# An encoder layer with two kinds of attention: projections as one stream through all head pairs, a shared bank for short score stretches, and a fixed order on three engines

## The chip, the cores and the metric

The kernel runs on one core of a Trainium2 chip. The metric is the device time of one execution in microseconds (us), the median of several. One execution was also profiled, and the trace below is of that one. The engines are PE (TensorE: matrix products and transposes), DVE (VectorE), ACT (ScalarE), POOL (GpSimd) and SP (SyncE, which issues transfers). Each runs its own instructions in the order of its own list, and stands still when the next one's data or room is not there.

## The reference

One encoder layer on two streams of tokens, `x_prompt` (1024 tokens, called R here) and `x_sample` (512 tokens, S), with shared weights. Eight heads of width 64 do neighbourhood attention on a grid (group a), eight do dilated window attention (group b).

```python
hn = rms_norm(x, g_attn)
proj = hn @ w_in
qa, ka, va, qd, kd, vd = jnp.split(proj, 6, axis=-1)
oa = neighbourhood_attention(heads(qa), heads(ka), heads(va), rpb)
od = dilated_attention(heads(qd), heads(kd), heads(vd), slopes)
mix = jnp.concatenate([rms_norm(oa, g_na), rms_norm(od, g_dil)], axis=-1)
x = x + mix @ w_out
hn = rms_norm(x, g_ffn)
return x + (jax.nn.silu(hn @ w_gate) * (hn @ w_up)) @ w_down
```

Inside each attention, a block of 128 queries meets its window of keys: scores, plus a table of biases and masks, softmax over the window, times the values.

## The kernel before

**Pairs and blocks.** Attention goes through 16 pairs: two heads of one group and one stream. Pairs 0 to 7 are those of R (b, a, b, a, ...), pairs 8 to 15 those of S in the same order. A pair of R has 16 blocks, eight of its first head and then eight of its second; a pair of S has four and four. `blocks_of(pi)` lists them, and `k.j` is the number of a block within its head.

**One block.** Scores are two sorts of product into a bank of PSUM, L698 with the high part of the keys and L699 with the low part (`sc`; in a b block of R a long stretch of 512 keys and a short one of 256, of which the short one had the name `sc2`; 384 keys in an a block of R; 512 and 256 in the b and a blocks of S). DVE adds the table and takes the minimum of the negated scores (L739, with the reading of its accumulator). ACT takes the exponential (L746). PE transposes the result (L756, bank `tp`), ACT copies it as 16-bit numbers (L760, the high part of `pT`), DVE computes what the copy lost (L761, the low part). PE multiplies with the values (L776), two blocks at a time, DVE adds up their pieces (L785), and after four blocks it takes the reciprocal and POOL scales and stores.

**Projections.** The queries, keys and values of the next pair are computed while a pair's blocks are (`qkv(pi)`, a generator; order v, q, k). Each product of an fp32 activation and an fp32 weight is three products of rounded halves (`mm3`, L155); the generator yields after every six, which is called a step here. A pair of R costs 24 steps, 144 matmuls of 512 columns; one of S 12 steps, 72 matmuls. Behind the matmuls come works of DVE, ACT and POOL: the sums `am` (L426) and low parts of v (L473), q (L539) and k (L508), ACT's high parts and copies, and, for b, copies at the borders (L411, L412).

**What sets the order.** `interleave()` writes one pair's blocks and the next pair's projections alternately: scores one block ahead, `dense.upto((j + DF) / n)` in the middle of block j and `dense.upto((j + 1) / n)` at its end, with `j` counted over all `n` blocks of the pair. That is only the order in which the program is written: the scheduler of the language then sets each engine's order, by data and by priorities, so that an engine's list can hold a later block's work ahead of an earlier one's. Only the opening (first loads and projections) is written in a fixed order. `bank()` hands out PSUM banks by name: 2 for projections (`mm`), 3 for scores (`sc`), 1 for values, 2 for transposes.

**Tables.** The bias tables of group a are built from `bias_e` tiles that `bias_load` loads and `bias_rows` (L332 to L339) shifts and writes back; they take their room in turn from the tag `p16`, which also serves the 16-bit values. Attention lies between some 67 and 795 us of the trace; after it follow the output projection's rest and the feed-forward part, which the change does not touch.

## Time and profile before

| what | value |
|---|---|
| median of 3 runs | 1977.09 us (1970.92 to 1977.22) |
| profiled execution | 1966.33 us, span of the trace 1964.3 us |
| PE busy over the span | 1842.0 us (94%) |
| DVE, ACT, POOL busy | 1321.1, 916.4, 844.1 us (67%, 47%, 43%) |
| PE's share of the chain that ended last | 74% |
| DVE's, DMA's share of it | 9%, 7% |

The span is the time from the first instruction of the trace to the last; the execution's own time is a little more. The busy shares are means over stages with different limits. The chain that ended last is followed back from the last instruction: at each step to what released it, or to the instruction before it on its engine. The granted clock in the rows below (PEclk) is TensorE's: 1.00 stands for its upper level of 2.4 GHz, 0.50 for its lower of 1.2 GHz.

### The profile page before, as it was taken

Reading aid. Unit: us, or ns where it says so; the run is one execution under the profiler, and the core shown is the slowest. Engines: PE = TensorE matmul, PEld = TensorE weight load, DVE = VectorE, ACT = ScalarE, POOL = GpSimd, SP = SyncE. Lnnn points to the kernel's source line nnn. Section 1 sums busy time; section 2 is a strip of 40 time slices with the busy share of each in tenths; the row PEclk is TensorE's granted clock in tenths of the full one; section 3 lists DMA queues with packets and bytes.
Section 4 is the critical chain, followed back from the end, with each engine's and each line's share of the span. In section 5 each row is a group of like instructions: output and inputs, shape, how many; then the busy total and the mean of one; then the engine's idle time right before and its main releaser. Section 6 shows DMA issues by size and latency. Waiting matters only on the chain.

```text
span 1964.3 us, 28970 instructions
## 1 busy us (share of the span) xinstructions
PE 1842.0 (94%) x10450; PEld 1609.9 (82%) x10450; DVE 1321.1 (67%) x2626; ACT 916.4 (47%) x1731; POOL 844.1 (43%) x690
## 2 busy tenths in 40 slices
PE   6889999898999998999899999879999997999998
PEld 4777777677777776788899999879999995877886
DVE  7566656656656567566976777877767665757765
ACT  5455557555566667443433333433333332324431
POOL 4323324232355551100666666656666543642110
PEclk9999999999899998999999999989999998999999
DMA  7623323232344455353354343334343448866642
GB/s 263 142 66 99 88 82 104 58 88 69 97 108 119 117 164 143 136 161 118 107 150 130 108 131 101 113 109 122 105 131 104 132 127 314 272 217 234 226 166 94
DMA packets 218943, 265.97 MB, mean 135 GB/s; under 512 B 59584, under 2 KB 163152, under 8 KB 218800
## 3 DMA queue, kind: packets, MB, share of 16 engines
q1 hardware_dynamic: 196176, 179.57, 30.4%
q0 software_dynamic: 22624, 84.56, 14.5%
q8 instruction: 82, 1.34, 0.3%
q14 instruction: 61, 0.50, 0.1%
HBM read 202.71 MB, written 51.41 MB: 129 GB/s over the span
## 4 chain that ended last, share of the span: by engine, by line
PE 74%; DVE 9%; DMA 7%; issue 4%; ACT 3%; POOL 2%; SPq 0%; DVEq 0%; POOLq 0%; ACTq 0%
PE acc L155 37%; PE yacc L155 11%; PE zacc L155 7%; PE mmacc L155 7%; PE pt L756 4%; PE pv L776 3%; PE sc L698 2%; DVE flo L1080 2%; PE sc L699 2%; DMA left<-hid_d 1%; DMA fraw<-in_w_up_dram 1%; POOL fs L1084 1%; DVE t L739 1%; PE pt L210 1%; DMA wq<-in_w_down_dram 1%
## 5 line engine op out<-in xcount | busy, mean ns | idle before, releaser
L155 PE MATMUL acc<-dhi,left 128*128 128x512 f32 x924 | 289.8, 394 | 16.6 <-ACT left L1254 14.0
L155 PE MATMUL acc<-hth,whi 128*128 128x512 f32 x576 | 233.5, 405 | 7.1 <-DVE kl L508 5.4
L155 PE MATMUL acc<-htl,whi 128*128 128x512 f32 x576 | 231.3, 401 | 1.0 <-POOL htl L294 0.5
L1080 DVE TENSOR_TENSOR flo<-fs,fhi 128x512 fp32r<-128x512 f32 x176 | 173.8, 991 | 86.2 <-ACT fhi L1079 85.1
L155 PE MATMUL acc<-hth,wlo 128*128 128x512 f32 x576 | 230.5, 400 | 0.1
L155 PEld LDWEIGHTS acc<-dhi,left 128*128 128x128 f32 x924 | 174.1, 189 | 57.8 <-ACT left L1254 15.3
L1079 ACT ACTIVATE fhi<-fs 128x512 fp32r<-128x512 f32 x176 | 109.5, 629 | 188.3 <-POOL fs L1084 81.4
L125 POOL TENSOR_TENSOR wlo<-wraw,whi 128x1024 fp32r<-128x1024 f32 x48 | 115.7, 2411 | 165.9 <-ACT whi L124 154.8
L155 PE MATMUL acc<-dlo,left 128*128 128x512 f32 x462 | 181.5, 393 | 0.0
L746 ACT ACTIVATE t<-t,mt 128x768 f32<-128x768 f32 (+3 forms) x192 | 138.1, 720 | 68.5 <-DVE mt L739 64.4
L760 ACT ACTIVATE pT<-pt 128x512 f16<-128x512 f32 (+2 forms) x256 | 118.8, 485 | 108.3 <-PE pt L756 107.1
L1084 POOL TENSOR_TENSOR fs<-fraw 128x512 f32<-128x512 f32 x88 | 131.6, 1510 | 83.6 <-DMA fraw<-in_w_up_dram 76.6
L1080 DVE TENSOR_TENSOR flo<-fraw,fhi 128x512 fp32r<-128x512 f32 x132 | 160.4, 1216 | 0.3 <-ACT fhi L1079 0.2
L1238 POOL TENSOR_TENSOR wq<-wq 128x512 f32<-128x512 f32 x55 | 92.3, 1689 | 156.7 <-DMA wq<-in_w_down_dram 124.5
L761 DVE SCALAR_TENSOR_TENSOR pT<-pt,pT 128x512 f16<-128x512 f32 (+2 forms) x256 | 136.8, 550 | 14.0 <-ACT pT L760 13.0
L1079 ACT ACTIVATE fhi<-fraw 128x512 fp32r<-128x512 f32 x132 | 82.9, 629 | 115.0 <-PE yacc L155 92.4
L155 PEld LDWEIGHTS acc<-hth,whi 128*128 128x128 f32 x576 | 109.9, 191 | 31.2 <-DVE kl L508 6.9
L756 PE MATMUL pt<-ident,t 128*128 128x128 f32 x768 | 125.6, 283 | 6.2 <-DVE pT L761 5.0
L1255 DVE TENSOR_TENSOR left<-left,left 128x1408 fp32r<-128x1408 f32 x42 | 74.4, 1773 | 83.8 <-ACT left L1254 83.8
L155 PEld LDWEIGHTS acc<-htl,whi 128*128 128x128 f32 x576 | 110.1, 191 | 24.9 <-DVE htl L294 2.1
L791 POOL TENSOR_TENSOR ob<-ob,den 128x256 f32<-128x256 f32 x48 | 29.6, 617 | 234.1 <-DVE ob L785 99.5
L1198 POOL TENSOR_TENSOR as<-a,as 128x384 f32<-128x384 f32 x66 | 89.0, 1348 | 91.9 <-DVE a L1187 72.5
(219 smaller groups left out, 4980.7 us busy)
## 6 DMA issues: line engine op xcount, KB each, us to landing
wq<-in_w_down_dram SPq DMA_DIRECT2D x132, 256.0 KB
hid_d<-as POOLq DMA_DIRECT2D x22, 1344.0 KB, 8.0
left<-hid_d SPq DMA_DIRECT2D x42, 704.0 KB
wraw<-in_w_in_dram POOLq DMA_DIRECT2D x46, 512.0 KB, 5.0
fraw<-in_w_gate_dram SPq DMA_DIRECT2D x45, 512.0 KB
fraw<-in_w_up_dram SPq DMA_DIRECT2D x45, 512.0 KB
tabb<-in_tabb_dram POOLq DMA_DIRECT2D x8, 800.0 KB, 4.9
xh<-x_d SPq DMA_DIRECT2D x12, 512.0 KB
```

Source lines behind the costliest of these rows:

```text
L125: eng.tensor_tensor(out=lo, in0=src, in1=hi.bitcast(F32), op=ALU.subtract))
L155: latest[0] = nc.tensor.matmul(out=out, lhsT=a, rhs=b, start=first and i == 0, stop=i == last, skip_group_check=not first)
L746: nc.scalar.activation(t, t, AF.Exp, bias=mt, scale=-1.0, accum_out=k.den)
L756: nc.tensor.transpose(out=pt[:, c * P:(c + 1) * P], in_=k.t[:, (c0 + c) * P:(c0 + c + 1) * P], identity=ident)
L760: nc.scalar.activation(hi, pt, AF.Copy, scale=16384.0)
L761: nc.vector.scalar_tensor_tensor(out=lo, in0=pt, scalar=16384.0, in1=hi, op0=ALU.mult, op1=ALU.subtract)
L1079: nc.scalar.activation(hi, src, AF.Copy)
L1080: nc.vector.tensor_tensor(out=lo, in0=src, in1=hi.bitcast(F32), op=ALU.subtract)
L1084: nc.gpsimd.tensor_tensor(out=o, in0=a, in1=b, op=op)
L1198: nc.gpsimd.tensor_tensor(out=part[n], in0=p, in1=q, op=op)
L1238: nc.gpsimd.tensor_tensor(out=src, in0=src, in1=other, op=q[1])
L1255: nc.vector.tensor_tensor(out=lo, in0=raw_lo, in1=hi.bitcast(F32), op=ALU.subtract)
```

## The change

`interleave()` and its class `Dense` go. In their place all blocks of all pairs stand in one list `todo`, and all projections in one generator `stream()`. `step(g)` writes block g: its softmax, the transposes, copies and low parts of the block before (`turn(pipe[-1])`), the sums and values of earlier ones, the scores of block g+1, and then as many steps of projections as `target(k.pi, k.j)` asks for, meant to run `LEAD` = 2 blocks ahead. Ahead of a new pair's first scores the stream is drained until that pair's projections are "whole". Where the pair whose projections stream (`at[0]`) is none of 4, 7, 15 and 16, the three engines PE, ACT and DVE keep the order in which the program is written (`manual_schedule`); that is while the blocks of pairs 0, 1, 2, 4, 5, 7 and 8 to 13 run. Pairs 3, 6, 14 and 15 are left to the scheduler.

Besides: the short stretch of a b block of R takes half of one bank of its own (`s2`), the halves in turn, and `sc` has two banks instead of three; the second head's low keys have two tiles in turn (`klow`), so that `held`, which delayed them, goes; the low parts of both heads are issued together (`lows`); the high part of v's second half comes three steps later; the `bias_e` tiles take the room of the tag `pT`; values are taken at odd `j`.

```diff
-TB, P16, PTB, OB = 3, 3, 3, 2
-BANKS = dict(mm=("mm", 2), sc=("sc", 3), pv=("pv", 1), tp=("tp", 2))
+TB, P16, PTB, OB = 3, 2, 3, 2
+BANKS = dict(mm=("mm", 2), sc=("sc", 2), s2=("s2", 1), pv=("pv", 1), tp=("tp", 2))
...
-            f = rb.tile([P, NA + 1, 32], F32, tag="p16", name="bias_e", bufs=P16)
+            f = rb.tile([P, NA + 1, 32], F32, tag="pT", name="bias_e", bufs=PTB)
...
-                    v_high_a(1)
+                    after(3, lambda: v_high_a(1))
...
-                res["kl"] = [z[:, :nx] for z in klow]
+                res["kl"] = [klow[i][:, :nx] for i in (0, 1 + pi % 2)]
...
-                sc = bank("sc", "sc2")
+                if "s2" not in heads:
+                    heads["s2"] = bank("s2", "s2")
+                sc = heads["s2"][:, k.j % 2 * 256:k.j % 2 * 256 + 256]
...
+    totals = [12 * st.nch for st, _, _ in pairs] + [11 + 8 * NO]
+    counts = [2 * st.nq for st, _, _ in pairs]
...
+    def target(pi, j):
+
+        base, j = sum(totals[1:pi + 1]), j + 1 + LEAD
+        if pi == len(pairs) - 1:
+            return base + totals[pi + 1] * j / (counts[pi] + LEAD)
+        if j <= counts[pi]:
+            return base + totals[pi + 1] * j / counts[pi]
+        n = counts[min(pi + 1, len(pairs) - 1)] + (LEAD if pi + 2 == len(pairs) else 0)
+        return base + totals[pi + 1] + totals[pi + 2] * (j - counts[pi]) / n
...
+    def step(g):
+        k = todo[g]
+        softmax(k)
+        if pipe:
+            turn(pipe[-1])
+        pipe.append(k)
+        while owed:
+            head_out(owed.pop())
+        if k.j % 2 and len(pipe) > LAG:
+            values(pipe[:2])
+            owed.append(pipe[1])
+            del pipe[:2]
+        if g + 1 < len(todo):
+            nxt = todo[g + 1].pi
+            while not done.get(nxt, {}).get("whole"):
+                advance()
+            scores(todo[g + 1])
+        if g + TL < len(todo):
+            tables(todo[g + TL])
+        while spent[0] < target(k.pi, k.j):
+            was = spent[0]
+            advance()
+            if spent[0] == was:
+                break
...
+    loose = (SQ, len(order) - 1, len(pairs) - 1, len(pairs))
+    g = 0
+    while g < len(todo):
+        with ExitStack() as fixed:
+            if at[0] not in loose:
+                fixed.enter_context(tc.manual_schedule(engines=core))
+            now = at[0] in loose
+            while g < len(todo) and (at[0] in loose) == now:
+                step(g)
+                g += 1
```

In the rows of order below, a name's number tells one use of a buffer from another, and `ISA` is the score operation that adds the table. DVE in the second head of pair 0, before (score operations are L739, low parts L761):

```order
L739 ISA t_1050,mt_1051<-sc_994,tabb_799 128x512
L739 ISA mt_1051 128x1
L739 ISA t_1050,mt_1053<-sc2_997,tabb_799,mt_1051 128x256
L739 ISA mt_1053 128x1
L761 SCALAR_TENSOR_TENSOR pT_981<-pt_982,pT_981 128x512
L761 SCALAR_TENSOR_TENSOR pT_981<-pt_989,pT_981 128x256
L739 ISA t_1105,mt_1106<-sc_1027,tabb_799 128x512
L739 ISA mt_1106 128x1
L761 SCALAR_TENSOR_TENSOR pT_1014<-pt_1015,pT_1014 128x512
L785 TENSOR_REDUCE ob_1012<-pv_718 128x128
L761 SCALAR_TENSOR_TENSOR pT_1014<-pt_1022,pT_1014 128x256
L739 ISA t_1105,mt_1108<-sc2_1030,tabb_799,mt_1106 128x256
```

And after (score operations L741, low parts L763):

```order
L741 ISA t_1037,mt_1038<-sc_1032,tabb_838 128x512
L741 ISA mt_1038 128x1
L741 ISA t_1037,mt_1040<-s2_557,tabb_838,mt_1038 128x256
L741 ISA mt_1040 128x1
L763 SCALAR_TENSOR_TENSOR pT_1043<-pt_1044,pT_1043 128x512
L763 SCALAR_TENSOR_TENSOR pT_1043<-pt_1051,pT_1043 128x256
L787 TENSOR_REDUCE ob_982<-pv_700 128x128
L790 RECIPROCAL den_751<-den_751 128x4
L741 ISA t_1066,mt_1067<-sc_1061,tabb_838 128x512
L741 ISA mt_1067 128x1
L741 ISA t_1066,mt_1069<-s2_557,tabb_838,mt_1067 128x256
L741 ISA mt_1069 128x1
```

Before, the scores of the blocks `t_1006`, `t_1050` and `t_1105` stand together, and the low parts `pT_981` and `pT_1014` belong to blocks three back. After, between the scores of two blocks stand always the two low parts of the block before the first of them.

ACT at the same place, before (exponentials are L746, copies L760):

```order
L746 ACTIVATE t_1050,den_955<-t_1050,mt_1053 128x768
L760 ACTIVATE pT_1014<-pt_1015 128x512
L760 ACTIVATE pT_1014<-pt_1022 128x256
L760 ACTIVATE pT_1080<-pt_1081 128x512
L746 ACTIVATE t_1105,den_955<-t_1105,mt_1108 128x768
L760 ACTIVATE pT_1080<-pt_1088 128x256
L746 ACTIVATE t_1153,den_1158<-t_1153,mt_1156 128x768
L760 ACTIVATE pT_1116<-pt_1117 128x512
L760 ACTIVATE pT_1116<-pt_1124 128x256
L760 ACTIVATE pT_1184<-pt_1185 128x512
L746 ACTIVATE t_1211,den_1158<-t_1211,mt_1214 128x768
```

And after (L748 and L762):

```order
L762 ACTIVATE pT_995<-pt_1003 128x256
L748 ACTIVATE t_1037,den_967<-t_1037,mt_1040 128x768
L762 ACTIVATE pT_1043<-pt_1044 128x512
L762 ACTIVATE pT_1043<-pt_1051 128x256
L748 ACTIVATE t_1066,den_967<-t_1066,mt_1069 128x768
L762 ACTIVATE pT_1072<-pt_1073 128x512
L762 ACTIVATE pT_1072<-pt_1080 128x256
L748 ACTIVATE t_1114,den_1119<-t_1114,mt_1117 128x768
L762 ACTIVATE pT_1121<-pt_1122 128x512
L762 ACTIVATE pT_1121<-pt_1129 128x256
L748 ACTIVATE t_1141,den_1119<-t_1141,mt_1144 128x768
```

Before, one to three pairs of copies stand between exponentials, and a pair of copies is also split by one. After, it is one exponential and the copies of one block in strict turn, and the block whose copies follow an exponential is the one before it.

PE at the end of pair 0, before; `acc` are projections, `sc` scores of pair 1, `pt` transposes of pair 0's last blocks:

```order
L155 MATMUL acc_1347<-hth_100,wlo_1246 128x512
L155 MATMUL acc_1347<-hth_100,whi_1245 128x512
L698 MATMUL sc_1341<-ka0_1147,qa0_879 128x384
L699 MATMUL sc_1341<-kl0_92,qa0_879 128x384
L155 MATMUL acc_1347<-htl_101,whi_1245 128x512
L155 MATMUL acc_1347<-hth_100,wlo_1246 128x512
L756 MATMUL pt_1227<-ident_69,t_1153 128x128 x2
L776 LDWEIGHTS pT_1184
L776 MATMUL pv_718<-vnb_463,pT_1184 128x64
L776 LDWEIGHTS pT_1184
```

And after; the rows left out are 56 further projection matmuls and one small product:

```order
L778 MATMUL pv_700<-vnb_465,pT_1200 128x64
L778 LDWEIGHTS pT_1200
L778 MATMUL pv_700<-vnb_465,pT_1200 128x128
L155 MATMUL acc_883<-hth_104,whi_638 128x512
L155 MATMUL acc_883<-htl_105,whi_638 128x512
L155 MATMUL acc_883<-hth_104,wlo_639 128x512
...
L155 MATMUL acc_1352<-htl_103,whi_1330 128x512
L155 MATMUL acc_1352<-hth_102,wlo_1331 128x512
L698 MATMUL sc_1361<-ka0_1309,qa0_846 128x384
L699 MATMUL sc_1361<-kl0_92,qa0_846 128x384
L758 MATMUL pt_1375<-ident_69,t_1223 128x128 x4
L758 MATMUL pt_1382<-ident_69,t_1223 128x128 x2
```

Before, the first scores of pair 1 stand amid the projections, and transposes and values of pair 0 behind them. After, 60 projection matmuls stand in one piece between the last values that pair 0's loop takes and the first scores of pair 1; in the eight blocks of the second head ahead of them PE's list has no projection matmul at all.

## Rows read from the trace of the kernel before

The windows of rows 1 run from the first score operation of a pair to that of another: pair 0, pair 2, pair 7, and pairs 8 to 13.

**Rows 1.** Windows: us; busy PE, PEld, DVE, ACT, POOL; PEclk; DMA share; GB/s.
```profile
67.00:148.00 81.00, 69.39 (x448) 55.47 (x447) 44.54 (x119) 42.39 (x83) 22.05 (x25) 0.96 0.52 117
202.10:278.70 76.60, 72.84 (x507) 59.03 (x507) 50.55 (x127) 44.71 (x91) 23.22 (x27) 0.96 0.27 71
534.10:588.40 54.30, 53.17 (x345) 42.67 (x345) 28.47 (x81) 34.47 (x77) 29.69 (x24) 1.00 0.42 107
588.40:742.20 153.80, 147.78 (x955) 118.80 (x953) 97.39 (x259) 102.79 (x229) 78.91 (x77) 0.99 0.50 136
```

**Rows 2.** Waits of TensorE for a bank: us in total, times, longest.
```profile
PE sc L698 <- DVE mt L739: 19.5, 23, 5.6
```

**Rows 3.** Timeline of VectorE, two score operations: start, us.
```profile
375.45 0.69 DVE L739 CUSTOM_DVE_ANT_0 t<-sc,tabb 128x512 f32<-128x512 f32 x1 [0.76 <-PE pt L756]
...
378.66 0.69 DVE L739 CUSTOM_DVE_ANT_0 t<-sc,tabb 128x512 f32<-128x512 f32 x1 [1.04 <-PE pt L756]
```

**Rows 4.** Groups by shape, 48 to 800 us: busy, mean ns; idle, releasers.
```profile
L761 DVE SCALAR_TENSOR_TENSOR pT<-pt,pT 128x512 f16<-128x512 f32 x96 | 65.2, 686 | 6.1 <-ACT pT L760 5.8
L739 DVE CUSTOM_DVE_ANT_0 t<-sc,tabb 128x512 f32<-128x512 f32 x96 | 65.1, 687 | 47.4 <-PE pt L756 46.7
L746 ACT ACTIVATE t<-t,mt 128x768 f32<-128x768 f32 x64 | 59.8, 934 | 51.7 <-DVE mt L739 50.0 <-DVE den L788 1.1
L760 ACT ACTIVATE pT<-pt 128x512 f16<-128x512 f32 x96 | 56.3, 594 | 37.3 <-PE pt L756 36.8
...
L785 DVE TENSOR_REDUCE ob<-pv 128x128 f32<-128x256 f32 x94 | 39.5, 420 | 26.8 <-PE pv L776 17.6 <-issue 8.5
L761 DVE SCALAR_TENSOR_TENSOR pT<-pt,pT 128x256 f16<-128x256 f32 x95 | 39.3, 416 | 4.1 <-ACT pT L760 3.9
L746 ACT ACTIVATE t<-t,mt 128x384 f32<-128x384 f32 x64 | 39.3, 614 | 7.2 <-DVE mt L739 5.7 <-DVE den L788 0.3
...
L760 ACT ACTIVATE pT<-pt 128x256 f16<-128x256 f32 x95 | 35.6, 377 | 38.5 <-PE pt L756 38.3
...
L739 DVE CUSTOM_DVE_ANT_0 t<-sc,taba 128x384 f32<-128x384 f32 x64 | 35.0, 553 | 49.1 <-PE pt L756 48.1 <-PE sc L699 0.5
L761 DVE SCALAR_TENSOR_TENSOR pT<-pt,pT 128x384 f16<-128x384 f32 x64 | 34.7, 548 | 3.7 <-ACT pT L760 3.4
...
L539 DVE SCALAR_TENSOR_TENSOR qa<-acc,qa 64x512 fp32r<-64x512 f32 x46 | 31.7, 688 | 22.7 <-ACT qa L535 21.9
...
L760 ACT ACTIVATE pT<-pt 128x384 f16<-128x384 f32 x64 | 30.2, 484 | 32.4 <-PE pt L756 32.0
...
L739 DVE CUSTOM_DVE_ANT_1 t<-sc,tabb,mt 128x256 f32<-128x256 f32 x48 | 22.9, 478 | 9.5 <-PE sc L699 9.2
L746 ACT ACTIVATE t<-t,mt 128x512 f32<-128x512 f32 x32 | 22.9, 719 | 5.7 <-DVE mt L739 5.2 <-DVE rox L111 0.4
...
L746 ACT ACTIVATE t<-t,mt 128x256 f32<-128x256 f32 x32 | 16.2, 506 | 3.9 <-DVE mt L739 3.5
L473 DVE SCALAR_TENSOR_TENSOR va<-vT,vsc,va 128x512 f16<-128x512 f32 x16 | 16.0, 1039 | 7.3 <-DMA vna<-va 6.7 <-ACT va L468 0.6
...
L739 DVE CUSTOM_DVE_ANT_0 t<-sc,taba 128x256 f32<-128x256 f32 x32 | 13.4, 420 | 17.2 <-PE pt L756 17.0
...
L426 DVE TENSOR_REDUCE am<-vT 128x1 f32<-128x1024 f32 x8 | 9.7, 1217 | 4.1 <-ACT vT L418 4.1
```

**Rows 5.** The chain that ended last: start us, us, work.
```profile
296.66 5.46 PE acc L155 x24
```

**Rows 6.** Two neighbouring windows in pair 2; columns as in rows 1.
```profile
235.30:242.10 6.80, 4.68 (x43) 3.32 (x43) 5.60 (x15) 6.67 (x14) 5.14 (x6) 1.00 0.25 78
242.10:248.90 6.80, 6.33 (x42) 5.14 (x39) 3.75 (x11) 2.81 (x7) 0.53 (x1) 0.50 0.44 140
```

**Rows 7.** Timeline of TensorE: its longest idle time in the first.
```profile
241.00 0.23 PE L776 MATMUL pv<-vnb,pT 128*128 128x128 f16 x1 [0.94 <-ACT pT L760]
```

**Rows 8.** Timeline of VectorE in the first pair.
```profile
81.21 0.93 DVE L334 TENSOR_TENSOR bias_e<-bias_e 128x736 f32<-128x736 f32 x1 [6.45 <-DMA bias_e<-in_rpbf_dram]
```

More of the change, by code (lines that the diff above doesn't have):

```diff
@@ L34 @@
 LAG = 3
-DF = 0.8
+LEAD = 2
 SQ = 4
@@ L215, in hymba_layer_kernel @@
     hT, st_out, halves = {}, {}, {}
-    klow = [rb.tile([P, TP + 256], F32R, tag=f"kl{i}", name=f"kl{i}", bufs=1) for i in range(2)]
-    held = []
+    klow = [rb.tile([P, TP + 256], F32R, tag=f"kl{i}", name=f"kl{i}", bufs=1) for i in range(3)]
     for i, z in enumerate(klow):
@@ L512, in low, with lows @@
                     borders(kl[i], own[i])
-            after(2, lambda: low(0))
-            if pi and ch == 0 and st.nch == 2:
-                held.append(lambda: low(1))
-            else:
-                after(2, lambda: low(1))
+            def lows():
+                low(0)
+                low(1)
+                if ch == st.nch - 1:
+                    res["whole"] = True
+            after(2, lows)
         def q_put(ch, acc):
@@ L896, in out_first @@
             yield from out_tile(i, NO)
-    class Dense:
-        def __init__(self, gen, total):
-            self.gen, self.total, self.spent = gen, total, 0
-        def upto(self, share):
-            while self.gen is not None and self.spent < share * self.total:
-                if next(self.gen, "end") == "end":
-                    self.gen = None
-                tick()
-                self.spent += 1
-        def rest(self):
-            if self.gen is not None:
-                run(self.gen)
-            flush()
@@ L915, in hymba_layer_kernel @@
-    pipe, owed = [], []
-    def interleave(pi, dense):
-        blocks = blocks_of(pi)
-        n = len(blocks)
-        tables(blocks[0])
-        scores(blocks[0])
-        for j, k in enumerate(blocks):
-            if j + 1 < n:
-                scores(blocks[j + 1])
-            while j == n - 2 and held:
-                held.pop()()
-            dense.upto((j + DF) / n)
-            softmax(k)
-            pipe.append(k)
-            while owed:
-                head_out(owed.pop())
-            if j % 2 == 0 and len(pipe) > LAG:
-                values(pipe[:2])
-                owed.append(pipe[1])
-                del pipe[:2]
-            if len(pipe) > 1:
-                turn(pipe[-2])
-            if j + TL < n:
-                tables(blocks[j + TL])
-            dense.upto((j + 1) / n)
-        dense.rest()
+    totals = [12 * st.nch for st, _, _ in pairs] + [11 + 8 * NO]
@@ new lines, in hymba_layer_kernel, with stream, advance @@
+    counts = [2 * st.nq for st, _, _ in pairs]
+    def stream():
+        for pi in range(1, len(pairs)):
+            at[0] = pi
+            for _ in qkv(pi):
+                yield
+        at[0] = len(pairs)
+        yield from out_first()
+    at = [1]
+    dense, spent = stream(), [0]
+    def advance(n=1):
+        for _ in range(n):
+            if next(dense, "end") == "end":
+                return
+            tick()
+            spent[0] += 1
+    def target(pi, j):
[6 more added lines that the diff above has]
+        return base + totals[pi + 1] + totals[pi + 2] * (j - counts[pi]) / n
@@ new lines, in hymba_layer_kernel @@
+    pipe, owed = [], []
+    todo = [k for pi in range(len(pairs)) for k in blocks_of(pi)]
+    def step(g):
[22 more added lines that the diff above has]
+                break
@@ L943, in hymba_layer_kernel @@
+    core = {mybir.EngineType.Activation, mybir.EngineType.DVE, mybir.EngineType.PE}
     run(qkv(0))
@@ L945, in hymba_layer_kernel @@
     flush()
-    for pi in range(len(pairs)):
-        if pi + 1 < len(pairs):
-            dense = Dense(qkv(pi + 1), 12 * pairs[pi + 1][0].nch)
-        else:
-            dense = Dense(out_first(), 11 + 8 * NO)
-        interleave(pi, dense)
+    for k in todo[:TL]:
+        tables(k)
+    scores(todo[0])
+    loose = (SQ, len(order) - 1, len(pairs) - 1, len(pairs))
[8 more added lines that the diff above has]
+                g += 1
+    for _ in dense:
+        tick()
+    flush()
     while owed:
```

## The prediction

> **What bounds the kernel now.** I read the view by windows first, cut at the first score operation of each pair. PE is busy for 72.84 of 76.60 us in pair 2, 53.17 of 54.30 in pair 7 and 147.78 of 153.80 in pairs 8 to 13, at a clock of 0.96 to 1.00; only pair 0 has more slack, 69.39 of 81.00, and DVE and ACT stand at half to two thirds [rows 1]. The reader should see that attention is bounded by PE, and that a change can win little more than PE's idle time, but can lose whatever new idle time it makes. One sort of that idle time is named by the view of waits: PE stood 19.5 us in 23 waits for a score bank that DVE had not read yet [rows 2]. Then I asked how fast the blocks go without projections: in the timeline of VectorE two such score operations of b blocks stand 375.45 and 378.66, so 3.21 us apart [rows 3].
>
> **The change part by part.**
>
> *Order on ACT and DVE.* The order of the program after the change shows a closed chain in the fixed parts. DVE's scores of block j free ACT's exponential of j; ACT's copies of block j-1 stand behind that exponential; DVE's low parts of j-1 need these copies; and DVE's scores of j+1 stand behind the low parts. Nothing of one round overlaps the next, but the second copy beside the first low part. Before, copies and low parts lagged by three blocks, and the pieces overlapped. The durations of one round [rows 4]: b block of R, scores 0.687 + 0.478, exponential 0.934, first copy 0.594, low parts 0.686 + 0.416, sum 3.80 us. a block of R: 0.553 + 0.614 + 0.484 + 0.548 = 2.20. b block of S: 0.687 + 0.719 + 0.594 + 0.686 = 2.69. a block of S: 0.420 + 0.506 + 0.377 + 0.416 = 1.72. To each I add 0.30: half a sum of values, 0.21 [rows 4], and 0.09 as an estimate for the reciprocal and the hand-overs, which no row shows alone. So 4.1, 2.5, 3.0 and 2.0 us, against 3.21 for the b block of R before. PE needs less: pair 2's 72.84 us without 144 projection matmuls at 5.46 / 24 = 0.2275 us [rows 5], so without 32.8, is 40.1, or 2.5 us a block. PE will wait for the chain in blocks without projections.
>
> *Where the projections go.* `target` takes `k.j`, which starts anew with each head. In the first head of a pair of R it rises to 24 * 10 / 16 = 15 steps, of which two were done ahead or lie behind the boundary; in the second it asks for nothing that is not already spent. PE's list confirms it: no projection in the second head, then 60 matmuls in one piece. So PE idles in the second head and must make up at the boundary. With the chain as pace, a pair takes its blocks, the DVE works of projections that stand in the chain, and the boundary.
>
> The DVE works in the first head of a pair of R: `am` 1.22, two low parts of v at 1.04, two of q at 0.69 [rows 4], and 0.9 of small ones (an estimate), 5.6 us. In a pair of S all but q are half as wide: I take 4.0. They are hidden only while PE is longer than the chain, and in the first head PE is about even with it: 2.5 + 78 * 0.2275 / 8 = 4.7 us a block, the chain 4.1 + 0.7.
>
> The boundary, b to a: 60 * 0.2275 = 13.65 us, less some 2.5 that the last blocks' softmax covers, and 0.4 for the first scores: 11.5. a to b: 54 * 0.2275 = 12.3, then the copies of k, low parts and borders that the first scores wait for, 1.2 + 0.7 + 1.3, and 0.5 for scores, less 1.5 covered: 14.5. In S 18 * 0.2275 = 4.1, with 1.2 + 0.7 + 0.7 behind it 6.7, less 2 or 1 covered: 4.7 and 5.7. The works behind the matmuls are priced like the copies and the low parts of q [rows 4]; what is covered is an estimate of half a chain.
>
> Pairs after: b of R 16 * 4.1 + 5.6 + 11.5 = 82.7; a of R 40 + 5.6 + 14.5 = 60.1; pair 7, which carries only a pair of S, 40 + 4.0 + 6.6 = 50.6; S 24 + 4.0 + 4.7 = 32.7 and 16 + 4.0 + 5.7 = 25.7, three of each 175.2. Against before [rows 1]: pair 0 +1.7, pairs 2 and 4 (like pair 2) +6.1 each, pairs 1 and 5 (like pair 7) +5.8 each, pair 7 -3.7, S +21.4: **+43.2**. Pairs 3, 6, 14 and 15 stay with the scheduler, and their blocks, projections and durations are the same: 0.
>
> *First blocks.* Right behind a pair's first block some 24 projection matmuls stand in PE's list, 5.5 us, and the transposes of that block wait behind them. That is longer than a round by 1.3 us in three b pairs of R, 2.8 in two a pairs, 1.6 in pair 7 (18 matmuls), and 2.2 and 3.5 in three pairs each of S: 28 us in all. Part of it is the time that the DVE works take anyway, so I take half, **+14**; bounds 0 and 28.
>
> *Banks and tiles.* The bank of the short stretch removes most of the 19.5 us of waits [rows 2], but the place of that wait is taken by the chain; 0 within the sum above. The halves of one bank make the scores of block j+1 wait for DVE's short score operation of j-1 or j, some 1.2 us into a round; PE arrives there later. A third tile of low keys and the later high part of v ease waits of DVE and ACT that lie off the path while PE is behind the chain: 0. `p16` with two buffers: a pair's v needs two at a time, and the next pair's come a pair later: 0, and a wait on them would show on ACT ahead of v's copies.
>
> *Opening.* The three `bias_e` operations no longer wait for `p16`. Before, one of them cost DVE 0.93 us behind 6.45 us of waiting for its load, in pair 0 [rows 8]. After, they stand in DVE's list in the opening, and their loads on SP ahead of pair 0, so that this wait moves to before the first scores. Bounds 0 and 8; I take **+5**. What pair 0 loses of it is in its 1.7 above.
>
> *Clock.* In pair 2 PE was busy for 4.68 of 6.80 us at the clock 1.00, and in the next 6.80 us the clock was at 0.50, though the longest idle time in the former was 0.94 us [rows 6, 7]. Half of 6.80, 3.4 us, is what one such fall costs where PE is the limit. After the change the second heads have PE busy for 2.5 of 4.1 us, a like share, in every fixed pair. Where PE waits for the chain a slow clock costs little, but the burst at the boundary is on the path. I take three more falls that count, **+10**; bounds 0 and twelve, 41. The Trainium skill ("TensorE: Matmul & The Clock Gate", section "HAM oscillation — how this bites in real kernels") puts such falls down to single long idle gaps, as in a wait for a transfer; idle times of under 1 us would then leave the clock alone, the term would be 0 and the sum 10 us lower. The trace of this kernel does not agree with that, so the row decides.
>
> **Sum**: 43.2 + 14 + 5 + 10 = +72 us. The durations come from the profiled execution (1966.33 us, span 1964.3), which is 10.8 us shorter than the median of the three runs, 1977.09. Nothing says that the difference lies in attention, so I add the 72 to the median: **2049 us**. On the profile's own time it would be 2038.
>
> **The rivals.**
>
> *A, the forecast*: the chain as pace, starved second heads and bursts: 2025 to 2075.
>
> *B, the clock and the first blocks cost all that they can*: opening 8, stalls 28, clock 41, with 43 from the chain +120, 2097. For it: every fixed pair has a second head with the busy share of [rows 6]. Against: pair 2 shows the fall, but its mean clock is still 0.96 [rows 1].
>
> *C, most of the added work is hidden*: half of the DVE works (five pairs at 5.6, seven at 4.0, together 56) runs while PE works through the first head's projections, no stalls, no opening, no falls: 43 - 28 = +15, 1992; with a few of these, to 2015. For it: PE and chain are about even there, so one of them hides the other.
>
> *D, the other side*: the round of the chain is no longer than PE's own work, PE gets back its idle time and nothing is lost. It decides if a b block of R in a second head goes at 2.5 us and the projections spread as before. The gain would be PE's idle time [rows 1]: 11.6 in pair 0, 3.8 twice, 1.1 three times, 6.0 in S, 28.5 us: 1948. For it: the waits for banks are gone [rows 2]. Against: the list shows no projections in second heads, and each part of the round waits for the one before it; five durations would have to overlap that cannot.
>
> That the change does not do what it says (projections two blocks ahead) is part of A: the order shows a head's numbering, not a pair's.
>
> **How the numbers follow.** A has 0.62, B 0.17, C 0.14, D 0.07. A measurement of this kernel can tell about 0.3%, 6 us, from no change. The range reaches from the bound of C to that of B, 1992 to 2097, which leaves out D and the outer ends of B and C. A's own range is 2025 to 2075. Faster by over 0.3%: D, 0.06. Within 0.3%: the remaining hundredth of D and the lowest of C, 0.03. Slower: 0.91.
>
> **What would show it.** In the timeline of VectorE the score operations of second heads of b pairs of R should stand 4.1 us apart (a: 2.5; S: 3.0 and 2.0), with low parts between them that wait for ACT's copies. PE's idle time in these heads should be put down to ACT and DVE, and a stretch of PE with 60 projection matmuls, 13 to 14 us at the full clock, should end each fixed pair of R but pair 7. The window of pair 2 should be 80 to 86 us, that of pair 5 58 to 63, and pairs 8 to 13 together 170 to 195. The waits of PE for scores' banks should fall below 5 us. The feed-forward part should be as before, within 3 us. I am wrong in the step on the chain if rounds are under 3.5 us; in the step on the projections if second heads have projection matmuls; in the clock if the clock stays over 0.97 in all these pairs or falls under 0.85.

## The result and the profile after

The changed kernel takes 2107.2 us (median, 2102.23 to 2109.23) against 1975.89 for the one before: 1.0673 times as long, interval 1.0647 to 1.0698, or **131 us more**. The forecast had the sign and the mechanism, and 72 us; its range ended at 2097. The profiled execution took 2102.23 us, its span is 2100.5.

The view by windows of the changed kernel, cut at the first score operations of pairs 0, 2, 7 and 8 to 13; in [rows 1] the window of pair 0 begins with its second block, at 67.0, and not with its first, at 47.7 (us; busy PE, PEld, DVE, ACT, POOL; PEclk; DMA share; GB/s):

```profile
58.00:164.40 106.40, 87.26 (x529) 70.27 (x529) 54.94 (x140) 48.18 (x94) 21.95 (x21) 0.91 0.25 67
229.50:322.00 92.50, 76.37 (x522) 61.95 (x522) 48.14 (x129) 44.80 (x91) 23.74 (x24) 0.94 0.22 60
605.00:655.80 50.80, 37.67 (x250) 29.36 (x250) 28.13 (x75) 26.46 (x63) 20.43 (x21) 0.90 0.35 89
655.80:871.30 215.50, 177.12 (x1011) 139.41 (x1010) 102.77 (x255) 106.13 (x230) 95.17 (x83) 0.92 0.35 89
```

PE is busy for 76.37 of 92.50 us in pair 2, where it was 72.84 of 76.60, and for 177.12 of 215.50 in pairs 8 to 13, where it was 147.78 of 153.80. The reader should see that PE's idle time went from 3.8 to 16.1 us in the one and from 6.0 to 38.4 in the other: PE is no longer what bounds these pairs. Its busy time grew too: the windows hold 15 and 56 more products than those of before, and the clock is 0.94 and 0.92 where it was 0.96 and 0.99.

The view of waits says for what the other engines stand (us in total, times, longest):

```profile
DVE pT L763 <- ACT pT L762: 240.0, 152, 9.1
ACT t L748 <- DVE mt L741: 231.3, 135, 4.5
...
PE s L698 <- DVE mt L741: 13.9, 22, 1.8
...
PE sc L698 <- DVE mt L741: 4.2, 6, 1.3
```

DVE's low parts wait 240 us for ACT's copies, and ACT's exponentials 231 us for DVE's scores; in the groups of [rows 4] the low parts of all shapes had 5.8, 3.9 and 3.4 us of such waits, the exponentials 50.0, 5.7, 5.2 and 3.5. PE's waits for a score bank, 19.5 us for all stretches before [rows 2], are now 4.2 for `sc` and 13.9 for the shared bank (`s`), 18.1 together.

The timeline of VectorE in the second head of pair 4, rows of two score operations and the low parts between them:

```profile
434.73 0.69 DVE L741 CUSTOM_DVE_ANT_0 t<-sc,tabb 128x512 f32<-128x512 f32 x1
...
437.70 1.02 DVE L763 SCALAR_TENSOR_TENSOR pT<-pt,pT 128x512 f16<-128x512 f32 x2 [1.64 <-ACT pT L762]
...
439.06 0.66 DVE L741 CUSTOM_DVE_ANT_0 t<-sc,tabb 128x512 f32<-128x512 f32 x1
```

And the timeline of ACT beside it:

```profile
436.16 0.94 ACT L748 ACTIVATE t<-t,mt 128x768 f32<-128x768 f32 x1 [2.16 <-DVE mt L741]
...
437.10 0.85 ACT L762 ACTIVATE pT<-pt 128x512 f16<-128x512 f32 x2
```

The round closes as forecast: scores from 434.73, exponential at 436.16 after 2.16 us of waiting for them, copies at 437.10, low parts at 437.70 after 1.64 us of waiting for the copies, next scores at 439.06. One round takes 4.33 us, the seven gaps of this head alternate between 3.9 and 4.3. Before, it was 3.21 [rows 3].

The stages against each other, from the starts of pairs' first score operations in VectorE's timeline:

| stage | before, us | after, us | difference | forecast with half of the first blocks' stalls |
|---|---|---|---|---|
| up to the first score operation of pair 0 | 47.7 | 58.0 | +10.3 | +5 |
| pair 0 | 100.3 | 106.4 | +6.1 | +2.3 |
| pairs 1, 5 | 54.1, 54.4 | 65.1, 64.9 | +21.5 | +14.4 |
| pairs 2, 4 | 76.6, 76.5 | 92.5, 86.7 | +26.1 | +13.5 |
| pairs 3, 6 | 46.0, 78.5 | 48.2, 83.2 | +6.9 | 0 |
| pair 7 | 54.3 | 50.8 | -3.5 | -2.9 |
| pairs 8 to 13 | 153.8 | 215.5 | +61.7 | +29.9 |
| clock, not placed in a pair | | | | +10 |
| sum up to 742.2 and 871.3 | 742.2 | 871.3 | +129 | +72 |

The windows do not hold the same work everywhere: that of pairs 8 to 13 has 455 projection matmuls after and 406 before, at 0.2275 us each [rows 5] some 11 us of PE's time. What lies behind the table, to the end of the trace, takes 1222.1 us before and 1229.2 after; the feed-forward part was forecast as before within 3 us, and why it is longer was not looked into. The loss lies where it was forecast, in the fixed pairs and the opening, and 31.8 of the 57 us that the forecast missed lie in the six pairs of S.

### The profile page after: what moved, and what is told of

Same layout as the page of the kernel before. It is cut to its first block, busy times and chain, and to the rows that moved or that the text cites. A ratio compares the mean times of both kernels' runs of the same rounds, so it can differ in the third digit from the quotient of the medians.

```text
span 2100.5 us, 28931 instructions
## 1 busy us (share of the span) xinstructions
PE 1889.2 (90%) x10450; PEld 1642.7 (78%) x10450; DVE 1334.3 (64%) x2626; ACT 913.9 (44%) x1731; POOL 845.1 (40%) x691
## 4 chain that ended last, share of the span: by engine, by line
PE 49%; DVE 7%; DMA 6%; issue 5%; ACT 4%; POOL 4%; SPq 0%; DVEq 0%; ACTq 0%; POOLq 0%
PE acc L155 19%; PE yacc L155 12%; PE zacc L155 8%; PE mmacc L155 7%; DMA wq<-in_w_down_dram 2%; POOL wlo L125 1%; POOL wq L1270 1%; DVE flo L1112 1%; DVE t L741 1%; ACT t L748 1%; ACT pT L762 1%; DMA left<-hid_d 1%; PE pt L210 1%; DMA hid_d<-as 1%; ACT ka L504 1%
## 5 line engine op out<-in xcount | busy, mean ns | idle before, releaser
L763 DVE SCALAR_TENSOR_TENSOR pT<-pt,pT 128x512 f16<-128x512 f32 (+2 forms) x256 | 137.1, 555 | 240.3 <-ACT pT L762 240.0
L155 PE MATMUL acc<-hth,whi 128*128 128x512 f32 x576 | 237.9, 413 | 6.1 <-ACT hth L290 5.4
L748 ACT ACTIVATE t<-t,mt 128x768 f32<-128x768 f32 (+3 forms) x192 | 138.4, 721 | 232.3 <-DVE mt L741 231.3
L155 PE MATMUL acc<-hth,wlo 128*128 128x512 f32 x576 | 234.8, 408 | 3.0 <-POOL wlo L125 2.7
L758 PE MATMUL pt<-ident,t 128*128 128x128 f32 x768 | 132.0, 296 | 73.5 <-DVE pT L763 37.7
L758 PEld LDWEIGHTS pt<-ident,t 128*128 128x128 f32 x768 | 95.4, 151 | 108.9 <-ACT t L748 48.2
L155 PEld LDWEIGHTS acc<-hth,wlo 128*128 128x128 f32 x576 | 112.3, 195 | 34.1 <-POOL wlo L125 8.9
```

Of the source, the lines that this page charges most:

```text
L155: latest[0] = nc.tensor.matmul(out=out, lhsT=a, rhs=b, start=first and i == 0, stop=i == last, skip_group_check=not first)
L748: nc.scalar.activation(t, t, AF.Exp, bias=mt, scale=-1.0, accum_out=k.den)
L758: nc.tensor.transpose(out=pt[:, c * P:(c + 1) * P], in_=k.t[:, (c0 + c) * P:(c0 + c + 1) * P], identity=ident)
L763: nc.vector.scalar_tensor_tensor(out=lo, in0=pt, scalar=16384.0, in1=hi, op0=ALU.mult, op1=ALU.subtract)
```

## The experiments

Each run has its own times of the kernel before, so what comes back or is added is taken from the difference of two ratios, times 1975.89 us; what comes back is counted from the changed kernel's 1.0673. The smaller edits of the change (the third tile of low keys, both low parts together, v's later high part, values at odd `j`) were not run alone.

**The stream by the pair's number.** The target gets the block's number within the pair.

```diff
-        while spent[0] < target(k.pi, k.j):
+        while spent[0] < target(k.pi, k.i * k.st.nq + k.j):
```

> The stream's target counts a block's number within the pair instead of within the head; nothing else differs from the changed kernel. Theory: nearly all of the 131 us comes from the starved second heads, the bursts at the boundaries and the clock that falls ahead of them; with projections spread over 16 blocks PE has 2.5 + 9 x 0.2275 = 4.5 us of work in a b block of R, more than the 4.1 us of the round, and the time is 1985 to 2005 us, the clock over 0.97. Rival (the closed round of ACT and DVE costs as such): the rounds stay the pace with the DVE works of projections in them, and the time is over 2050 us.

Measured: 2033.5 us, 1.0304 (1.0289 to 1.0320). Window of pair 2:

```profile
218.70:296.50 77.80, 68.80 (x487) 55.72 (x487) 46.07 (x126) 45.82 (x92) 25.76 (x25) 0.98 0.24 66
```

77.8 us against 92.5, with PE busy for 68.8. About 73 us come back, more than half of the loss, less than I expected (1985 to 2005 us): second heads now have projections, but the rounds without them stay at 3.9 to 4.3 us. Neither theory is right alone.

**No fixed order.** All pairs are left to the scheduler; the target still goes by the head's number.

```diff
-            if at[0] not in loose:
+            if False:
```

> The changed kernel with every pair left to the scheduler, the target still by the head's number. The pairs that are loose in the changed kernel lost 2 and 5 us, so if fixing the order is what makes the head's number costly, 2010 to 2035 us. If the order of the source (bursts) costs as such, whoever sets the engines' lists: over 2070 us.

Measured: 1986.3 us, 1.0064 (1.0048 to 1.0080): 120 of 131 us come back, more than either theory gave. Window of pair 2:

```profile
214.80:292.40 77.60, 72.89 (x501) 58.53 (x501) 46.54 (x129) 44.57 (x86) 26.01 (x27) 1.00 0.27 75
```

PE is busy for 72.89 of 77.60 us, as before the change. The uneven stream costs little when the scheduler may move the work of all three engines; it costs in the fixed order.

**Exponential behind the copies.** `softmax` loses its last line, and `step` does it after `turn`.

```diff
-        nc.scalar.activation(t, t, AF.Exp, bias=mt, scale=-1.0, accum_out=k.den)
+        k.mt = mt
+
+    def soft_exp(k):
+        nc.scalar.activation(k.t, k.t, AF.Exp, bias=k.mt, scale=-1.0, accum_out=k.den)
...
         if pipe:
             turn(pipe[-1])
+        soft_exp(k)
```

> The changed kernel with each exponential written behind the copies of the block before it instead of ahead of them; target by the head's number as before. If the closed round sets the pace of the second heads, rounds of b blocks of R fall from 4.1 to 2.6 to 2.9 us, those of a from 2.5 to 1.7 to 2.0, and 40 to 70 us come back: 2035 to 2065. If the boundaries and the clock hold most of the loss, less than 20 us come back: over 2087.

Measured: 2025.3 us, 1.0268 (1.0252 to 1.0283): 80 us come back, more than the 70 that I gave at most. In the timeline of VectorE two neighbouring score operations in the second head of pair 4 are now 2.87 us apart:

```profile
384.78 0.69 DVE L741 CUSTOM_DVE_ANT_0 t<-sc,tabb 128x512 f32<-128x512 f32 x1
...
387.65 0.66 DVE L741 CUSTOM_DVE_ANT_0 t<-sc,tabb 128x512 f32<-128x512 f32 x1
```

The other gaps of that head are 2.3 to 3.6. The closed round is shown: turning two lines round in ACT's order is enough to open it.

**Filling PE's idle time.** In the second heads of fixed pairs the score products are done twice.

```diff
-            nc.tensor.matmul(out=out, lhsT=qh[:, qs], rhs=kx, start=True, stop=False)
-            nc.tensor.matmul(out=out, lhsT=qh[:, qs], rhs=lx, start=False, stop=True)
+            for _ in range(2 if k.i and k.pi not in (3, 6, 14, 15) else 1):
+                nc.tensor.matmul(out=out, lhsT=qh[:, qs], rhs=kx, start=True, stop=False)
+                nc.tensor.matmul(out=out, lhsT=qh[:, qs], rhs=lx, start=False, stop=True)
```

> The changed kernel, but in the second heads of the fixed pairs each product of scores is done twice into the same bank (same result, work for idle time of PE; about 0.6 to 1.0 us a block). If the clock that falls in the second heads and is low in the bursts costs on the path: the mean clock rises from 0.955 to over 0.97 and 15 to 30 us come back in spite of more work, 2077 to 2092. If the clock costs nothing on the path: within 5 us of 2107, or up to 15 us longer where PE is late for the round.

Measured: 2105.4 us, 1.0673 (1.0656 to 1.0691). Pairs 8 to 13:

```profile
655.70:870.70 215.00, 178.33 (x1077) 140.80 (x1077) 105.26 (x261) 107.27 (x233) 98.85 (x87) 0.99 0.35 90
```

The clock there rose from 0.92 to 0.99, over the whole kernel from 0.955 to 0.974, and the window is 215.0 us instead of 215.5. Pairs 8, 10 and 12 take the same to 0.1 us in both runs, so in the rounds the lower clock stretched work that PE had time for, and the added products cost nothing. At two boundaries, where the clock had been low, it did cost. From the last score operation of pairs 9 and 11 to the first of the next pair, in the changed kernel:

```profile
715.40:725.30 9.90, 8.44 (x37) 6.56 (x37) 2.17 (x6) 4.18 (x8) 5.47 (x5) 0.86 0.31 90
784.80:795.80 11.00, 9.56 (x37) 7.36 (x37) 2.16 (x7) 4.18 (x8) 5.45 (x5) 0.77 0.30 84
```

And with the doubled products:

```profile
715.20:723.90 8.70, 7.25 (x37) 5.42 (x37) 2.26 (x7) 4.19 (x8) 5.49 (x5) 1.00 0.32 95
783.40:792.10 8.70, 7.32 (x37) 5.49 (x37) 2.23 (x7) 4.19 (x8) 5.50 (x5) 1.00 0.33 87
```

With 37 products each, they take 8.7 us at the clock 1.00 instead of 9.9 and 11.0. The boundary behind pair 13, which leads into a pair of the scheduler's, is 2.9 us longer there, so that the sum hides it.

**Both edits**: the pair's number and the exponential behind the copies.

> The changed kernel with both edits: the target by the block's number within the pair, and each exponential behind the copies of the block before. Alone the first gave back 74 us of 131 and the second 82. Theory: both fight the same loss (PE's idle time in second heads and what is made up at the boundaries), but with rounds near 2.7 us and projections in all of them PE is the limit again, and what is left is the works of the keys at the boundaries and the opening: 1980 to 2000 us. Rival: a fixed order costs something in every block whatever it is, since each late result stops all that stands behind it: over 2010 us.

Measured: 1961.2 us, 0.9933 (0.9909 to 0.9957): less than the kernel before, by 13 us, and below the 1980 to 2000 of my theory. Together the edits give back 146 us, where alone they gave 73 and 80: they add up to within 7 us. Windows of pair 2 and of pairs 8 to 13:

```profile
202.00:271.10 69.10, 66.57 (x492) 55.94 (x493) 45.84 (x126) 45.37 (x92) 26.00 (x26) 1.00 0.30 74
569.90:733.60 163.70, 157.51 (x999) 127.39 (x998) 94.54 (x255) 104.14 (x230) 91.68 (x82) 1.00 0.43 116
```

Pair 2 takes 69.1 us where it was 76.6, with PE busy for 66.57 of them at the clock 1.00. Pairs 8 to 13 are at 163.7, still over the 153.8 of before; ahead of the last block of pairs 8 to 12 the score operations are 6 to 8 us apart, and the boundary behind pair 13 takes 9.6. The rival, a cost of every fixed order, falls for the b pairs of R and stays open for S.

**Pair's number, no fixed order.** The two edits of the first two experiments together.

> The changed kernel with the target by the pair's number and every pair left to the scheduler. With the head's number the scheduler gave 1986. If it undoes the uneven writing by itself: 1982 to 1990. If the even stream, two blocks ahead, still gives it something: 1965 to 1980.

Measured: 1969.5 us, 0.9970 (0.9952 to 0.9987): 19 us under the head's number with the scheduler, so an even stream helps there too, and 6 us under the kernel before.

**The bias tiles' room, alone on the kernel before.**

```diff
-            f = rb.tile([P, NA + 1, 32], F32, tag="p16", name="bias_e", bufs=P16)
+            f = rb.tile([P, NA + 1, 32], F32, tag="pT", name="bias_e", bufs=PTB)
```

> The kernel before with only the bias tiles' room moved from p16 to pT. In the changed kernel the three operations on them stand ahead of the first scores, which start 10 us later (7 us with the scheduler). If that edit makes the shift: the first score operation comes 5 to 8 us later than 47.7, pair 0 loses its wait of 6.5 us, and the time is within 4 us of 1973, since one pays for the other. Rival (the shift is paid in full): 1978 to 1982.

Measured: 1986.3 us, 1.0065 (1.0044 to 1.0087), 13 us more, over both bounds that I gave. The timeline of VectorE has the first score operation at 58.37, where it was 47.7:

```profile
58.37 0.69 DVE L739 CUSTOM_DVE_ANT_0 t<-sc,tabb 128x512 f32<-128x512 f32 x1 [1.73 <-PE sc L699]
```

So this line makes the whole shift of the opening. Pair 0 takes back 7 of the 10.7 us (93.2 instead of 100.3). The two profiled executions are 23 us apart; the rest came in pairs 3, 6 and 7 (10.9), in pairs 8 to 13 (6.3) and behind them, where nothing was edited, and is not explained.

**The shared bank, alone on the kernel before.** `sc` two banks, `s2` one in halves, as in the diff of the change.

> The kernel before with only the scores' banks changed: two for the long stretches, one shared by the halves of the short ones. If the 19.5 us of PE's waits for a score bank lie on the path: 1958 to 1967. If another wait takes their place (the halves, or the transposes): 1970 to 1977.

Measured: 1983.1 us, 1.0050 (1.0026 to 1.0075). The wait of PE, by the view of waits:

```profile
PE sc L698 <- DVE mt L741: 10.7, 19, 1.9
...
PE s L698 <- DVE mt L741: 8.8, 1, 8.8
```

The wait for `sc` fell from 19.5 us to 10.7, but PE stands 8.8 us once for the shared bank, in pair 0: together 19.5 again. So the halves took the wait's place, as the second theory had it. The kernel got 10 us longer, which neither theory gave: pair 0 takes 4.6 us more, pair 3 takes 52.9 instead of 46.0, and the scheduler's lists differ all over attention, so that the rest is not explained.

**Three variants of the faster kernel** (both edits, 1961.2 us). Pair 3 in the fixed order too:

```diff
-    loose = (SQ, len(order) - 1, len(pairs) - 1, len(pairs))
+    loose = (len(order) - 1, len(pairs) - 1, len(pairs))
```

> The kernel with both edits (1961 us), and pair 3 in the fixed order too (the scheduler orders pairs 6, 14 and 15 alone). With the scheduler pair 3 took 51.8 us from first score to first score there, the fixed pairs 1 and 5 of the same kind 54.4 and 51.2. If a fixed order is as good as the scheduler's once the rounds are short: 1957 to 1965. If the scheduler fills PE better: 1965 to 1972.

Measured: 1976.2 us, 1.0017 (1.0001 to 1.0034), 17 us more, over both bounds that I gave. Pair 3 takes 61.6 us instead of 51.8: there the scheduler fills PE better, which is busy for 53.7 us of 61.6 in the fixed order and for 49.0 of 51.8 in the scheduler's.

The bias operations behind the fourth block of pair 0, in the room of the keys' tag:

```diff
+                if g == 4:
+                    bias_rows(loaded)
```

> The kernel with both edits (1961 us), with the bias tiles in the room of the keys' tag and the three DVE operations on them behind the fourth block of pair 0, not ahead of the first scores. If the opening's shift of 7 to 11 us is due to them and is on the path: the first score operation comes at 47 to 51 instead of 55.8 and the time is 1952 to 1958. If pair 0 takes back what the opening gives (the operations, their loads and stores beside its first blocks): 1959 to 1964.

Measured: 1985.1 us, 1.0047 (1.0029 to 1.0065). The first scores start at 47.5, as expected, but the timeline of VectorE has the operations like this:

```profile
83.90 0.93 DVE L333 TENSOR_TENSOR bias_e<-bias_e 128x736 f32<-128x736 f32 x1
98.57 0.93 DVE L333 TENSOR_TENSOR bias_e<-bias_e 128x736 f32<-128x736 f32 x1 [13.74 <-DMA bias_e<-in_rpbf_dram]
112.52 0.93 DVE L333 TENSOR_TENSOR bias_e<-bias_e 128x736 f32<-128x736 f32 x1 [13.02 <-DMA bias_e<-in_rpbf_dram]
```

DVE stands 13.74 and 13.02 us for loads that come late, and all scores stand behind it: pair 0 loses 27 us for the 8 won ahead of it, and the kernel is over both bounds that I gave. In a fixed order a late transfer is not stepped around.

Three score banks instead of the shared one (the old lines of the diff):

> The kernel with both edits (1961 us), with three score banks in turn for long and short stretches, as in the kernel before, instead of two and a shared one. On the kernel before, the shared bank alone made it 10 us longer. If in the fixed order a score bank is free in time either way: 1958 to 1964. If the waits of PE for a bank come back: 1966 to 1976.

Measured: 1959.8 us, 0.9926 (0.9905 to 0.9946), no difference to 1961.2. PE's wait, for all stretches (3.4 and 5.5 us for `sc` and the shared bank in the run with both edits):

```profile
PE sc L698 <- DVE mt L739: 4.0, 6, 1.1
```

In this order a bank is free in time either way; the shared bank neither pays nor costs.

**One engine free at a time**, in the changed kernel with nothing else altered.

```diff
-    core = {mybir.EngineType.Activation, mybir.EngineType.DVE, mybir.EngineType.PE}
+    core = {mybir.EngineType.Activation, mybir.EngineType.DVE}
```

> The changed kernel with PE's order left to the scheduler, ACT and DVE fixed, target by the head's number. The round of ACT and DVE stays at 4.1 us in b blocks of R; of the projections that are written at the boundary, PE's list has some 24 of 60 in the second head. If the loss is mostly made by ACT and DVE: over 2070. If PE's fixed list makes most of it: under 2040.

> The changed kernel with ACT's order left to the scheduler, PE and DVE fixed. ACT's list then has the copies of block j-1 ahead of the exponential of j, as in the edit by hand, which took 2025. If the closed round hangs on ACT's order: 2010 to 2035. If DVE's or PE's order closes it as well: over 2060.

> The changed kernel with DVE's order left to the scheduler, PE and ACT fixed. The scores of j+1 may then stand ahead of the low parts of j-1, which takes these (1.1 us in a b block of R) out of the round, but not ACT's exponential and first copy: rounds near 3.0 instead of 4.1. If so: 2045 to 2075. If DVE's order does not matter: over 2090.

Measured: PE free 2146.2 us, 1.0868 (1.0827 to 1.0909); ACT free 2061.8, 1.0436 (1.0393 to 1.0480); DVE free 2040.4, 1.0339 (1.0292 to 1.0386). Freeing DVE gives back 66 us, and the time is 5 us under the bound that I gave: the score operations of a second head of a b pair then come two by two, in pair 2 its seven gaps sum to 23.2 us instead of 28.9, so the round is open there too. Freeing ACT gives back 47 and lies in the rival's bounds, but not for the rival's reason: the score operations of second heads are 2.2 to 3.1 us apart in b pairs of R but for the first gap of each (4.2 to 4.3), so the round is open there, as with the edit by hand. In pairs of S, what it loses against that edit lies at first blocks, 7.8 to 9.5 us where the edit by hand had 6.6; what it loses in R was not traced. Freeing PE alone costs 39 us more, so PE's list by itself gives nothing back. A likely reason, not shown, is that its list then holds projections and scores in an order made for other times than those of the two fixed engines. Pairs 8 to 13 with PE free:

```profile
673.70:906.00 232.30, 196.17 (x1009) 146.39 (x1009) 102.34 (x255) 105.47 (x230) 94.52 (x83) 0.84 0.33 85
```

232.3 us instead of 215.5, at a clock of 0.84 with PE busy for 196 us. With 1009 products against 1011, PE is busy 19 us longer. The low clock lies at boundaries there, behind pair 10 for example, where 12.7 us stand against 9.0:

```profile
779.10:791.80 12.70, 11.04 (x48) 8.47 (x48) 5.65 (x9) 5.58 (x11) 5.98 (x6) 0.60 0.43 110
```

How much of the 39 us is the clock and how much the list was not separated.

## Why the forecast was right in kind and wrong in size

*Order on ACT and DVE.* Right: rounds of 3.9 to 4.3 (forecast 4.1), 2.2 to 2.7 (2.5), 2.7 to 3.1 (3.0) and 1.8 to 2.2 us (2.0). The run with the exponential behind the copies shows that this round, and not the fixed order as such, costs: 80 us. Those with ACT or DVE free, which open it too, give 47 and 66, but change more than the round.

*Where the projections go.* Right: second heads had none, and the pair's number gave back 73 us. It is a term beside the round: alone the edits give 73 and 80, together 146, 15 more than the loss. The head's number costs 73 us with the round closed and 66 with it open, but 19 where the scheduler orders all pairs. So missing projections hurt mostly where the engines cannot go ahead, whatever the round is.

*First blocks.* This step failed: "Part of it is the time that the DVE works take anyway, so I take half, **+14**; bounds 0 and 28." The stall is paid in full, 14 us more. The timeline of VectorE in pair 10 (b of S) shows all its score operations, the works at the boundary, and the first score operation of pair 11:

```profile
725.30 0.69 DVE L741 CUSTOM_DVE_ANT_0 t<-sc,tabb 128x512 f32<-128x512 f32 x1
...
731.94 0.68 DVE L741 CUSTOM_DVE_ANT_0 t<-sc,tabb 128x512 f32<-128x512 f32 x1
...
734.66 0.68 DVE L741 CUSTOM_DVE_ANT_0 t<-sc,tabb 128x512 f32<-128x512 f32 x1
...
739.51 0.68 DVE L741 CUSTOM_DVE_ANT_0 t<-sc,tabb 128x512 f32<-128x512 f32 x1
...
743.85 0.69 DVE L741 CUSTOM_DVE_ANT_0 t<-sc,tabb 128x512 f32<-128x512 f32 x1
...
746.91 0.68 DVE L741 CUSTOM_DVE_ANT_0 t<-sc,tabb 128x512 f32<-128x512 f32 x1
...
749.63 0.68 DVE L741 CUSTOM_DVE_ANT_0 t<-sc,tabb 128x512 f32<-128x512 f32 x1
...
752.76 0.66 DVE L741 CUSTOM_DVE_ANT_0 t<-sc,tabb 128x512 f32<-128x512 f32 x1
...
756.20 3.03 DVE L472 SCALAR_TENSOR_TENSOR va<-vT,vsc,va 128x256 f16<-128x256 f32 x2 [0.66 <-ACT va L467]
760.32 1.41 DVE L507 TENSOR_TENSOR kl<-acc,ka 64x512 fp32r<-64x512 f32 x2 [1.09 <-ACT ka L504]
761.76 0.42 DVE L741 CUSTOM_DVE_ANT_0 t<-sc,taba 128x256 f32<-128x256 f32 x1
```

Rounds without projections take 2.7 to 3.1 us, as forecast (743.85 to 752.76). The first gap, 6.64 us, is the one with 24 projection matmuls ahead of the transposes. All seven gaps sum to 27.5 us (27.6 and 27.1 in pairs 8 and 12); 7 * 3.0 for the rounds, 4.0 for the works and the whole stall of 2.2 make 27.2. In an a pair of S it is 23.0 against 14 + 4.0 + 3.5. In R the fifteen gaps of pairs 2 and 4 sum to 70.7 and 68.9 against 15 * 4.1 + 5.6 + 1.3 = 68.4, those of pairs 1 and 5 to 46.8 and 47.4 against 37.5 + 5.6 + 2.8 = 45.9.

*The boundary.* This term was mis-sized, and by more, 33 us in all. In S it was "4.7 and 5.7" us over a round in S, 7.7 in both from last to first score operation. Here 752.76 to 761.76 is 9.0 us; behind pairs 9, 11 and 13 it was 9.9, 11.0 and 16.5. PE's timeline has 24 projection matmuls there, not 18, and I had counted half of the works: the timeline of ACT has four copies of k in a row, not two, and DVE's low parts of k for both heads wait for them.

```profile
757.87 2.42 ACT L504 ACTIVATE ka<-acc 64x512 fp32r<-64x512 f32 x4 [1.30 <-PE acc L155]
```

2.42 us of copies stand where 1.2 were priced, and 1.41 of low parts where 0.7 was. The low parts of v ahead of them are not what the scores wait for, since DVE still waits 1.09 us for ACT behind them. Stalls in full (8.5 us more) and boundaries (18 us more) make up most of the 31.8 us that the S pairs had over their forecast. Of the 18 us, 8.8 are at the last boundary, which leads into a pair of the scheduler's and holds 48 projection matmuls, and 3.5 are the low clock behind pairs 9 and 11. In R the boundaries of the pairs 0, 1, 2, 4 and 5 took 17.5 to 21.8 us where the forecast has 15.6 and 17.0 with a round, that of pair 7 took 10.2 instead of 9.1: 15 us more.

*Opening.* Mis-sized: +5 against +10.3, over the bound of 8 (in the other runs with the tiles in the room of `pT` the first scores start at 54.6 to 59.2). The run with the tiles' room alone shows the cause; in it pair 0 got 7 us shorter, in the changed kernel 6.1 longer. The forecast's +1.7 for pair 0 set 16 rounds against the window of [rows 1], which holds 15 blocks; from the second block on pair 0 took 88.7 us against 81.0.

*Pairs left to the scheduler.* "their blocks, projections and durations are the same: 0" was +6.9 in pairs 3 and 6. Their blocks are the same, but not the order in which they are written; that this is the cause was not shown.

*Clock.* Too high: +10 was taken, and what shows on the path is 1.2 and 2.3 us at the boundaries behind pairs 9 and 11, and 1.6 behind pair 0 (19.5 us at the clock 0.92, 17.9 with the doubled products, at 1.00). Most of the falls lie in second heads, where PE has time. In the changed kernel's windows of pair 4, in its second head, ahead of its boundary and across it, the clock is 1.00, 0.76 and then 1.00:

```profile
417.90:428.10 10.20, 6.02 (x53) 4.64 (x54) 6.25 (x20) 3.69 (x9) 2.06 (x3) 1.00 0.06 14
...
431.00:439.20 8.20, 6.38 (x49) 5.56 (x48) 4.63 (x15) 3.57 (x8) 0.00 (x0) 0.76 0.00 0
439.20:456.90 17.70, 16.30 (x94) 13.13 (x92) 7.50 (x14) 8.83 (x16) 5.95 (x6) 1.00 0.33 93
```

It fell in the starved head, where a slower PE is still in time, and was back for the burst. That the falls come without a long stop of PE was right again, since in the first of these windows, just ahead of the fall, PE is busy for 6.02 of 10.20 us and its longest idle time is 1.83:

```profile
422.04 0.88 PE L758 MATMUL pt<-ident,t 128*128 128x128 f32 x6 [1.83 <-DVE pT L763]
```

The run with doubled scores kept the clock up and won nothing in the whole.

*Banks.* Waits "below 5 us" hold for `sc` (4.2), not with the shared bank's 13.9; together they are hardly less than before. In the faster form of the kernel the shared bank has no price, as the run with three banks shows; in the changed kernel itself this was not tried.

My rival B came nearest to the size with 2097, but the clock, the largest of what it adds to A's chain, was a wrong cause, so that its nearness is luck; its stalls of 28 in full were right. D's condition, "the round of the chain is no longer than PE's own work", is what both edits brought about: 69.1 us in pair 2.

## What to carry to other kernels

When a fixed order is built, draw the round through all engines: if each engine's next work stands behind another's last, the durations add up, and swapping two lines on one engine (here an exponential and the copies of the block before) can open it. A counter that paces one stream against another must run over the same loop as the stream; here it began anew with each head, and half of each pair went without its cover. In an estimate, price a boundary with all works of both heads, take a stall behind a burst in full, and charge a low clock only where PE is what the path waits for.

## What the runs showed of the hardware that was not expected

TensorE's mean clock rose from 0.92 to 0.99 in pairs 8 to 13 with more products in the idle time, at 215.0 and 215.5 us: the mean clock of a stretch does not say what it costs. Where the low clock fell into the rounds it cost nothing; where it fell into a boundary, with the same 37 products, it cost 1.2 and 2.3 us.
